# Steps 1 to 3 of the first product in a fused diffusion block: the next adaLN unit moved in front of the product with the activations' low half

## The chip, the cores and the metric

The kernel runs on one core of one Trainium2 chip. The metric is the device time of one execution in microseconds (us), the median of several runs. The engines named below are TensorE (PE in the profile; PEld is its loading of weights), VectorE (DVE), ScalarE (ACT), GpSimd (POOL) and the queue of SyncE (SP), which issues nearly all loads.

## The reference, cut to what matters

Two layers work on 256 latent tokens and 256 context tokens of width 1024. The change lies at the very start of the first layer: the adaLN map, the modulation of the tokens by it, and the first product of the Conformer module.

```python
def adaln(cvec, w, b):
    return jnp.split(jax.nn.silu(cvec) @ w + b, 6, axis=-1)

def modulate(x, shift, scale):
    return x * (1 + scale) + shift

def conformer_conv(u, rows, w_pw1, b_pw1, ...):
    a = u @ w_pw1 + b_pw1
    a = a[..., :CONV_DIM] * jax.nn.sigmoid(a[..., CONV_DIM:])
    ...
...
sh1, sc1, g1, sh2, sc2, g2 = adaln(c[:, None, :], ada_w[i], ada_b[i])
csh1, csc1, cg1, csh2, csc2, cg2 = adaln(c_ctx, ada_w[i], ada_b[i])
u = modulate(h, sh1, sc1)
uc = modulate(hc, csh1, csc1)
```

## The kernel before, in words

Context and latent tokens lie side by side as 512 columns, with the 1024 features in eight slabs of 128 partitions (`DT = 8`). Products are made in halves: each fp32 operand is split into a high part, rounded to the matmul's format, and a low part, the rest, and a product is three matmuls: high weight by high activation, high weight by low activation, low weight by high activation (`mm3`, lines 185, 188 and 189). `split` makes the halves of a weight (ScalarE casts the high one, line 154, VectorE subtracts to get the low one, line 155).

**The first product** is accumulated over the eight slabs in four blocks of 128 output columns, 0 to 3, each in a PSUM bank of its own (`ps0`); all four stay open over the eight steps. Step f needs the slab's scale and shift, and these come out of the adaLN weights step by step, in a chain:

- `start0(f)` (line 630) issues three loads on SP's queue (a 1 MB block of the adaLN weights into one of three buffers `raw`, the slab's part of the first weights, 256 KB, into one of five buffers `F`, the slab of x, 256 KB), then makes the adaLN *unit*: eight products on TensorE, 16 matmul records at line 342, into the PSUM bank `fl`. VectorE copies the bank out (line 646).
- `start1(f)` (line 648) splits the slab's weights, adds up the four partial sums of the unit with a matmul, the *fold* (line 350, into `ln`), turns them into shift and scale on VectorE (lines 655 and 656), and makes the modulated slab `u[f]` with `affine_split` (line 599): the high half on ScalarE and, for slabs 0 to 3, half of it on VectorE (lines 607 and 604), the same values in fp32 on VectorE (line 611), and last the low half, by a subtraction on VectorE (line 613).
- `start2(f, ms)` (line 672) makes the three matmuls of slab f for the blocks `ms`.

In step 0 the products of block 0, 1 and 2 are issued one by one by `part(ms, k)` (line 746): k = 0 is high by high, k = 1 low weight by high activation, k = 2 high weight by low activation. There part 2 comes behind the unit of slab 1.

In steps 1 to 3 the order on TensorE is: block 0 (three matmuls), the unit of slab f + 1, block 1, the fold of slab f + 1, blocks 2 and 3. The unit of slab 5 follows at the end of step 3; from step 4 on, the unit is two slabs ahead, and stands at the end of the step before. The order on TensorE and of the loads on SP's queue is pinned as written here (`keep_in_program_order`, and `pin[0]` for the units, folds and first matmuls of each `mm3`). The order on VectorE and ScalarE is not: the compiler of the kernel chooses it by priorities and a simulated time, held only by the edges that `issue_after` draws. So a chain of small additions (`foldg`, lines 787 and 789) with lowered priority has been put between step 1's low half and the next unit's copy, and a chain of sines (lines 682 to 695) among the splits that follow the first product.

After step 7 the other products of the Conformer module follow, and then the rest of the two layers; TensorE has work without a pause, and loads are issued when a buffer comes free.

Of the kernel before, what the change touches and what calls it, by code (L numbers as in the profile page):

```python
# [71 lines left out]
def hybrid_kernel(ctx: ExitStack, tc: tile.TileContext, xT, vecs_d, taps_d, bdw_d, ada0_w, ada_w, wg_d, pw1a, pw1, pw2, w1_0, w2_0,  # L72
                  w1_1, w2_1, up_x, up_z, wv, wo, bo_d, wk, wq, wqT, wdown, rows_d, out):
    nc = tc.nc
# [10 lines left out]
    def nm(s):  # L85
        uid[0] += 1
        return f"{s}_{uid[0]}"
# [13 lines left out]
    def psum(tag="mm"):  # L101
        return pp.tile([P, 512], F32, tag=tag, name=nm(tag), bufs={"mm": 3, "ln": 2, "fl": 1, "cv": 2}[tag])
# [81 lines left out]
    def mm3(ps, wh, wl, xh, xl, start, stop):  # L184
        a = nc.tensor.matmul(ps, wh, xh, start=start, stop=False)  # L185
        if pin[0]:
            tc.keep_in_program_order(a)
        nc.tensor.matmul(ps, wh, xl, start=False, stop=False)  # L188
        lastmm[0] = nc.tensor.matmul(ps, wl, xh, start=False, stop=stop).ins  # L189
# [30 lines left out]
    def kcol(w, kt):  # L220
        if isinstance(w[0], list):
            w, kt = (w[0][kt // 4], w[1][kt // 4]), kt % 4
        return w[0][:, kt * P:(kt + 1) * P], w[1][:, kt * P:(kt + 1) * P]
# [115 lines left out]
    def ada_mm(ps, blocks, v=0, first=True, last=True, kts=range(DT)):  # L339
        for kt in kts:  # L340
            j = kt % 4
            a = mark_unit[0] = nc.tensor.matmul(ps[32 * j:32 * j + 32], cs[:, kt, 14 - 2 * v:46 - 2 * v], blocks[kt],  # L342
                                 start=first and kt < 4, stop=last and kt >= 4, tile_position=(0, 32 * j))
            if pin[0]:
                tc.keep_in_program_order(a)
# [275 lines left out]
    x, u = [], []  # L621
    lastload = [None]
    KO0 = 4
    ps0 = [psum("cv" if m == 3 else "mm") for m in range(KO0)]
# [3 lines left out]
    st = {}  # L628

    def start0(f):  # L630
        t = X()
        raw = wp.tile([P, 2048], F32, tag="raw", name=nm("raw"), bufs=3)
        wr = F()
        loads = [(raw, ada0_w[f]), (wr[:, :KO0 * P], pw1a[f]), (t, xT[f * P:(f + 1) * P, :])]
        if f == 0:
            loads += [(bdw[:, 0:C], taps_d)]
        for d_, s_ in loads:
            lastload[0] = tc.keep_in_program_order(nc.sync.dma_start(d_, s_)).ins
        if f == 4:
            lastload[0] = tc.keep_in_program_order(nc.sync.dma_start(vecs[:, NV0:], vecs_d[:, NV0:])).ins  # L640
        x.append(t)
        ps = psum("fl")[:, :2 * P]
        ada_mm(ps, [raw[:, kt * 2 * P:(kt + 1) * 2 * P] for kt in range(DT)])
        sb = F()[:, :2 * P]
        with tc.issue_after(folded):
            st[f] = wr, sb, nc.vector.tensor_copy(sb, ps).ins

    def start1(f, then=lambda: None):
        if f:
            with tc.issue_after(st[f][2]), tc.issue_after(lastaff[0]):  # L650
                w = split_w(st[f][0][:, 0:KO0 * P])
        tr = ada_fold(st[f][1], 2 * P, tag="ln")
        then()
        with tc.issue_after(lastsub[0]) if f else nullcontext():
            nc.vector.tensor_scalar(sh1[:, :, f], tr[:, 0:2], vecs[:, o0 + f:o0 + f + 1], None, op0=ALU.add)
            sc_ = nc.vector.tensor_scalar(sc1[:, :, f], tr[:, 2:4], vecs[:, o0 + DT + f:o0 + DT + f + 1], 1.0,
                                          op0=ALU.add, op1=ALU.add)
        u.append((U(F32R), U(F32R)))
        if f:
            affine_split(*u[f], x[f], sc1, sh1, f, f < 4)  # L660
        else:
            def first_w():
                nonlocal w
                with tc.issue_after(lasthi[0]):
                    w = split_w(st[f][0][:, 0:KO0 * P])
                return lastsub[0]

            w = None
            affine_split(*u[f], x[f], sc1, sh1, f, True, first_w)
        st[f] = w  # L670

    def start2(f, ms):
        for m in ms:
            mm3(ps0[m], *kcol(st[f], m), *u[f], f == 0, f == DT - 1)
# [33 lines left out]
    keep = tc.keep_in_program_order  # L708
# [34 lines left out]
    start1(0, lambda: taps(banks))  # L743
    taps_out(banks)

    def part(ms, k):
        for m in ms:
            w_, x_ = kcol(st[0], m), u[0]
            keep(nc.tensor.matmul(ps0[m], w_[k == 1], x_[k == 2], start=k == 0, stop=False))

    part((0, 1), 0)
    part((0, 1), 1)
    part((2,), 0)
    part((2,), 1)
    start0(1)
# [2 lines left out]
    part((2,), 2)  # L758
    start2(0, (3,))
    for f in range(1, DT):  # L760
        start2(f, (0,))
        if f in (1, 2, 3):
            start0(f + 1)
            start2(f, (1,))
            start1(f + 1)
            start2(f, (2, 3))
        else:
            if f + 1 < DT:
                start1(f + 1)
            start2(f, (1, 2, 3))  # L770
        if 3 <= f and f + 2 < DT:
            start0(f + 2)
# [1380 lines left out]
```

## Time and profile before

| what | value |
|---|---|
| median of 3 runs | 1657.6 us (1657.56 to 1658.04) |
| the profiled execution | 1657.58 us, with a span of 1655.9 us |
| mean granted TensorE clock | 0.999 |
| ScalarE busy | 727.8 us (44%) |
| GpSimd busy | 14.3 us (1%) |
| read from HBM | 286.47 MB |

The span is the time from the first to the last record of the core; the rest of the execution's time lies around it. A timeline row gives the start and the length in us, the engine and line, the operation, output<-input with the tile names of the program, the shapes, and in brackets the idle time of the engine before it and what ended it. A row of waits gives who waited for whom, the total in us, how often, and the longest. A row of windows gives the stretch, its length, the busy time of each engine in it with its count, the granted clock, the share of the DMA engines and their GB/s. A matmul's length is modelled and overlaps the next one's, so the pace of matmuls is read from their starts.

### The profile page before, as it was taken

How to read it: one execution, taken by the hardware profiler on the slowest of the kernel's cores; microseconds unless marked ns; L12 is line 12 of the kernel's file. 1: busy time of each engine (PE TensorE's matmuls, PEld its weight loads, DVE VectorE, ACT ScalarE, POOL GpSimd, SP SyncE). 2: the span in 40 equal slices, each digit the busy share in tenths (PEclk: the TensorE clock that was granted, in tenths of full speed). 3: DMA queues.
4: the chain of work that ended last, by engine and by line, in shares of the span. 5: the costliest groups of instructions: out<-in, count | busy, mean ns of one | idle time of the engine just before them, and what ended most of it. 6: DMA issues, size and time to landing. Idle time of an engine off the chain costs nothing.

```text
span 1655.9 us, 22678 instructions
## 1 busy us (share of the span) xinstructions
PE 1642.1 (99%) x8818; PEld 1352.3 (82%) x8818; DVE 1045.7 (63%) x1884; ACT 727.8 (44%) x1170; POOL 14.3 (1%) x65
## 2 busy tenths in 40 slices
PE   8999999999999999999999999999999999999998
PEld 6665998888888998877787899888878888878887
DVE  6655895666535776762254753553489776776677
ACT  4313562232324475642233533442478654555453
POOL 0000000000000000000000000000000000000001
PEclk9999999999999999999999999999999999999999
DMA  8765313444324065557774852553466655685552
GB/s 342 252 228 220 115 64 122 150 139 147 118 102 153 9 233 190 190 194 278 283 247 151 293 179 86 178 192 143 151 226 220 212 212 205 237 288 182 178 188 92
DMA packets 80635, 305.81 MB, mean 185 GB/s; under 512 B 12012, under 2 KB 30352, under 8 KB 50576
## 3 DMA queue, kind: packets, MB, share of 16 engines
q1 hardware_dynamic: 58064, 288.07, 49.5%
q10 hardware_dynamic: 22464, 16.30, 3.1%
q8 instruction: 69, 1.13, 0.3%
q14 instruction: 38, 0.31, 0.1%
HBM read 286.47 MB, written 17.86 MB: 184 GB/s over the span
## 4 chain that ended last, share of the span: by engine, by line
PE 95%; DVE 2%; DMA 1%; ACT 1%; issue 0%; DVEq 0%; SPq 0%; ACTq 0%
PE mm L185 18%; PE mm L188 17%; PE mm L189 17%; PE mm L200 7%; PE mm L201 4%; PE mm L216 3%; PE mm L218 3%; PE mm L217 3%; PE fl L342 2%; PE cv L216 2%; PE cv L217 1%; PE cv L218 1%; PE ln L185 1%; PE cv L964 1%; PE ln L188 1%; PE fl L852 1%
## 5 line engine op out<-in xcount | busy, mean ns | idle before, releaser
L155 DVE TENSOR_TENSOR wl<-raw,wh 128x1024 fp32r<-128x1024 f32 x344 | 418.4, 1221 | 247.3 <-ACT wh L154 243.0
L154 ACT CAST wh<-raw 128x1024 fp32r<-128x1024 f32 x344 | 358.5, 1051 | 470.1 <-PE mm L188 247.3
L188 PE MATMUL mm<-u,wh 128*128 128x512 f32 (+1 forms) x805 | 290.6, 361 | 2.0 <-DVE u L613 2.0
L185 PE MATMUL mm<-u,wh 128*128 128x512 f32 (+1 forms) x677 | 242.1, 358 | 0.0
L189 PE MATMUL mm<-u,wl 128*128 128x512 f32 (+1 forms) x677 | 239.7, 354 | 0.0
L188 PEld LDWEIGHTS mm<-u,wh 128*128 128x128 f32 x805 | 152.0, 189 | 25.2 <-DVE u L613 3.5
L185 PEld LDWEIGHTS mm<-u,wh 128*128 128x128 f32 x677 | 127.8, 189 | 24.1 <-issue 4.7
L189 PEld LDWEIGHTS mm<-u,wl 128*128 128x128 f32 x677 | 127.9, 189 | 17.8
L216 PE MATMUL mm<-wh,xl 128*128 128x512 f32 x256 | 101.2, 395 | 0.8 <-ACT wh L154 0.8
L185 PE MATMUL mm<-xm,wh 128*128 128x512 f32 x256 | 101.0, 395 | 0.0
L217 PE MATMUL mm<-wh,xl 128*128 128x512 f32 x256 | 100.0, 391 | 0.0
L189 PE MATMUL mm<-xm,wl 128*128 128x512 f32 x256 | 99.7, 389 | 0.0
L218 PE MATMUL mm<-wl,xl 128*128 128x512 f32 x256 | 99.4, 392 | 0.2 <-DVE wl L155 0.2
L185 PE MATMUL mm<-hid,wh 128*128 128x512 f32 (+1 forms) x256 | 93.3, 364 | 0.0
L189 PE MATMUL mm<-hid,wl 128*128 128x512 f32 (+1 forms) x256 | 92.8, 363 | 0.0
L188 PE MATMUL mm<-hid,wh 128*128 128x512 f32 (+1 forms) x256 | 92.8, 363 | 0.0
L200 PE MATMUL mm<-x,wh 128*128 128x512 f32 x232 | 81.1, 398 | 0.0
L188 PE MATMUL mm<-qq,wh 128*128 128x272 f32 x256 | 73.9, 289 | 0.0
L185 PE MATMUL mm<-qq,wh 128*128 128x272 f32 x256 | 73.5, 288 | 0.0
L189 PE MATMUL mm<-qq,wl 128*128 128x272 f32 x256 | 73.5, 288 | 0.0
L200 PE MATMUL mm<-u,wh 128*128 128x512 f32 x192 | 68.6, 399 | 0.0
L1207 DVE SCALAR_TENSOR_TENSOR x<-mm,ada,x 128x256 f32<-128x256 f32 x64 | 28.5, 479 | 63.1 <-PE mm L189 63.1
(563 smaller groups left out, 3245.8 us busy)
## 6 DMA issues: line engine op xcount, KB each, us to landing
raw<-w SPq DMA_DIRECT2D x64, 1024.0 KB, 4.8
raw<-wo SPq DMA_DIRECT2D x32, 1024.0 KB, 4.9
raw<-ada_w SPq DMA_DIRECT2D x22, 1024.0 KB, 6.3
ar<-ada_w SPq DMA_DIRECT2D x80, 256.0 KB, 3.7
raw<-wv SPq DMA_DIRECT2D x16, 1024.0 KB, 7.5
raw<-wqT SPq DMA_DIRECT2D x16, 1024.0 KB, 6.2
raw<-wq SPq DMA_DIRECT2D x16, 1024.0 KB, 5.8
raw<-wk SPq DMA_DIRECT2D x16, 1024.0 KB, 4.9
```

Source lines behind the costliest of these rows:

```text
L154: c = nc.scalar.copy(hi, src)
L155: lastsub[0] = nc.vector.tensor_tensor(lo, src, hi.bitcast(F32), op=ALU.subtract).ins
L185: a = nc.tensor.matmul(ps, wh, xh, start=start, stop=False)
L188: nc.tensor.matmul(ps, wh, xl, start=False, stop=False)
L189: lastmm[0] = nc.tensor.matmul(ps, wl, xh, start=False, stop=stop).ins
L200: todo = [lambda s_, e_: nc.tensor.matmul(ps, wh, r[0], start=s_, stop=e_), lambda s_, e_: nc.tensor.matmul(ps[:, :n], wl, r[0][:, :n], st ...
L201: lambda s_, e_: nc.tensor.matmul(ps[:, :n], wl, r[0][:, :n], start=s_, stop=e_)]
L216: nc.tensor.matmul(ps, xh, wh, start=start, stop=False)
L217: nc.tensor.matmul(ps, xl, wh, start=False, stop=False)
L218: nc.tensor.matmul(ps, xh, wl, start=False, stop=stop)
L342: a = mark_unit[0] = nc.tensor.matmul(ps[32 * j:32 * j + 32], cs[:, kt, 14 - 2 * v:46 - 2 * v], blocks[kt], start=first and kt < 4, stop=l ...
L1207: nc.vector.scalar_tensor_tensor(res[m][:, sl_], p_, g[:, m:m + 1], res[m][:, sl_], op0=ALU.mult, op1=ALU.add)
```

## The change

In steps 1 to 3 block 0 is no longer done as a whole ahead of the unit of the next slab. Its products of the high activation half (high weight, then low weight) stay ahead of it; its product with the activations' low half comes behind it, ahead of block 1. For this `part` takes the slab as an argument. The three matmuls are the same; the low weight's product now comes second and not third. Steps 4 to 7 keep their order.

```diff
-    def part(ms, k):
+    def part(ms, k, f=0):
         for m in ms:
-            w_, x_ = kcol(st[0], m), u[0]
-            keep(nc.tensor.matmul(ps0[m], w_[k == 1], x_[k == 2], start=k == 0, stop=False))
+            w_, x_ = kcol(st[f], m), u[f]
+            keep(nc.tensor.matmul(ps0[m], w_[k == 1], x_[k == 2], start=k == 0 and f == 0, stop=False))
...
     for f in range(1, DT):
-        start2(f, (0,))
         if f in (1, 2, 3):
+            part((0,), 0, f)
+            part((0,), 1, f)
             start0(f + 1)
+            part((0,), 2, f)
             start2(f, (1,))
             start1(f + 1)
             start2(f, (2, 3))
         else:
+            start2(f, (0,))
             if f + 1 < DT:
                 start1(f + 1)
             start2(f, (1, 2, 3))
```

## Prediction

> **What bounds the kernel now.** I read the page's head first, then the list of what TensorE waited for over the whole span, then the first 45 us by timeline and by windows.
>
> ```profile
> span 1655.9 us, 22678 instructions
> PE 1642.1 (99%) x8818; PEld 1352.3 (82%) x8818; DVE 1045.7 (63%) x1884; ACT 727.8 (44%) x1170; POOL 14.3 (1%) x65
> ```
>
> TensorE is busy for 1642.1 of 1655.9 us. The list of its waits, whole span:
>
> ```profile
> PE mm L188 <- DVE u L613: 2.0, 3, 0.8
> PE fl L342 <- DMA raw<-ada_w: 1.2, 1, 1.2
> PE cv L179 <- DVE ones L138: 1.1, 1, 1.1
> PE mm L216 <- ACT wh L154: 0.8, 1, 0.8
> ```
>
> These are its four longest. The first is the change's target: three times, in steps 1, 2 and 3, the product with the low half (line 188) stood waiting for VectorE to finish that half (line 613). It is the largest wait that TensorE has, and still only 2.0 us. So the question is small: how much more than 2.0 us goes with it, and does any of it get lost before the end.
>
> The windows from each adaLN unit's start to the next one's (units 2 to 6):
>
> ```profile
> 16.85:22.15 5.30, 4.69 (x34) 2.96 (x33) 3.65 (x11) 1.11 (x2) 0.00 (x0) 1.00 1.01 393
> 22.15:27.46 5.31, 4.68 (x33) 2.96 (x32) 3.12 (x8) 1.11 (x2) 0.00 (x0) 1.00 1.05 412
> 27.46:31.17 3.71, 3.71 (x31) 2.48 (x30) 2.10 (x6) 0.98 (x2) 0.00 (x0) 1.00 1.02 407
> 31.17:35.57 4.40, 4.40 (x34) 3.04 (x33) 3.33 (x8) 2.23 (x5) 0.53 (x3) 1.00 1.03 409
> ```
>
> A step of the same work takes 5.30 and 5.31 us where the stall sits in it, and 4.40 us later, where none does (31.17:35.57). The granted clock is 1.00 in all four, so no clock goes into the sum. The DMA share is 1.0 throughout: the loads run at the limit of what this stage moves, about 400 GB/s, and that has to be watched.
>
> **The change, part by part.** The order of TensorE, step 1 in full and step 2's stall:
>
> ```profile
> 14.93 0.50 PE L185 MATMUL mm<-u,wh 128*128 128x512 f32 x1
> 16.19 0.50 PE L188 MATMUL mm<-u,wh 128*128 128x512 f32 x1 [0.75 <-DVE u L613]
> 16.53 0.40 PE L189 MATMUL mm<-u,wl 128*128 128x512 f32 x1
> 16.85 1.07 PE L342 MATMUL fl<-raw,cs 128*32 128x256 f32 x16
> 17.85 0.50 PE L185 MATMUL mm<-u,wh 128*128 128x512 f32 x1
> 18.19 0.40 PE L188 MATMUL mm<-u,wh 128*128 128x512 f32 x1
> 18.43 0.39 PE L189 MATMUL mm<-u,wl 128*128 128x512 f32 x1
> 18.65 0.50 PE L350 MATMUL ln<-fold,F 128*128 128x2 f32 x4
> 19.02 0.47 PE L185 MATMUL mm<-u,wh 128*128 128x512 f32 x1
> ...
> 20.48 0.40 PE L185 MATMUL mm<-u,wh 128*128 128x512 f32 x1
> 21.49 0.50 PE L188 MATMUL mm<-u,wh 128*128 128x512 f32 x1 [0.61 <-DVE u L613]
> 21.82 0.40 PE L189 MATMUL mm<-u,wl 128*128 128x512 f32 x1
> 22.15 1.07 PE L342 MATMUL fl<-raw,cs 128*32 128x256 f32 x16
> ```
>
> Nothing is removed and nothing added: the three matmuls of block 0 stay, and the unit's 16 records stay. What moves is the unit, from behind the stalled product to in front of it. The starts give the pace: a matmul after a wait or after a unit is followed 0.34 us later (16.19 to 16.53, 17.85 to 18.19), any other one 0.24 or 0.22 us later (18.19 to 18.43, 18.43 to 18.65), a low weight's product is followed by a unit after 0.32 us (16.53 to 16.85), a unit by a product after 1.00 us (16.85 to 17.85), and a fold by a product after 0.37 us (18.65 to 19.02).
>
> *Step 1.* High by high starts at 14.93 as before, since nothing ahead of it changes. Low weight by high activation follows at 15.27, the unit of slab 2 at 15.27 + 0.32 = 15.59, against 16.85: 1.26 us earlier. The product with the low half comes at 16.59.
>
> *Steps 2 and 3.* From unit to unit the new order is: unit 1.00; the low-half product 0.34; block 1, 0.24 + 0.24 + 0.22 = 0.70; fold 0.37; blocks 2 and 3, 1.46 (19.02 to 20.48); high by high 0.23 (the pace of blocks 1 to 3); low weight's product 0.32. Sum 4.42 us, beside the 4.40 of the undisturbed window. Units 3 and 4 then start at 20.01 and 24.43, against 22.15 and 27.46.
>
> *To unit 5.* Before, 3.71 us lie between units 4 and 5. After, the low-half product of block 0 lies there too: 3.71 + 0.24 = 3.95. Unit 5 starts at 28.38 and not at 31.17: **2.79 us** earlier. From there the order is the old one. The 2.79 is 2.0 of idle time, plus what the rows of idle time do not count: the wait begins at a matmul's modelled end, not at the pace of 0.23, and the matmul after each wait is a slow one.
>
> *Does the low half come in time?* The other engines of the chain, step 1 to 2:
>
> ```profile
> 15.44 0.69 DVE L613 TENSOR_TENSOR u<-S,u 128x512 fp32r<-128x512 f32 x1
> 16.05 0.17 DVE L787 TENSOR_TENSOR foldg<-ident 128x16 f32<-128x16 f32 x1
> 16.25 1.22 DVE L789 TENSOR_TENSOR foldg<-foldg,ident 128x16 f32<-128x16 f32 x6
> 17.99 0.42 DVE L646 COPY F<-fl 128x256 f32<-128x256 f32 x1 [0.52 <-PE fl L342]
> 18.33 0.68 DVE L155 TENSOR_TENSOR wl<-F,wh 128x512 fp32r<-128x512 f32 x1
> ...
> 19.58 0.60 ACT L607 ACTIVATE u<-x,sh1p,sc1p 128x256 fp32r<-128x256 f32 x1 [3.57 <-DVE sc1p L656]
> ...
> 20.74 0.69 DVE L613 TENSOR_TENSOR u<-S,u 128x512 fp32r<-128x512 f32 x1
> ```
>
> In step 1 the low half ends at 16.13, and the product now wants it at 16.59. In step 2 it ends 2.78 us after the fold's start (18.65 to 21.43). The new fold starts at 16.59 + 0.34 + 0.70 = 17.63, the low half ends at 20.41, and the product wants it at 20.01 + 1.00 = 21.01: 0.60 us of room. The high half ends 1.53 us after the fold's start (20.18), so at 19.16; high by high wants it at 15.59 + 1.00 + 0.34 + 0.70 + 0.37 + 1.46 = 19.46: 0.30 us of room, the smallest on this path. The low weights end 0.36 us after the fold's start (19.01), long ahead of their product, although it now comes second.
>
> *What the unit's new place makes wait.* The product with the low half, and behind it blocks 1 to 3 and the fold, now also stand behind the wait of the unit for its load. Before, only blocks 1 to 3 and the fold did.
>
> *What stood under the stall.* In step 1 VectorE filled its pause with seven `foldg` additions, 16.05 to 17.47, and the copy of the unit came behind them at 17.99. The copy trails the unit's start by 1.14 us, so it now wants to run at 16.73. If all seven additions stay ahead of it, it runs at about 17.40 to 17.82, and the fold at 17.88, not 17.63: 0.25 us lost, once. If they go behind, nothing or some tenths. I take 0.1, so **2.7 us** in all.
>
> *The loads.* Issue times, and us from that issue to landing, for the small weights of slab 2, then the blocks of units 4 and 5:
>
> ```profile
> 6.64 0.33 SPq L638 DMA_DIRECT2D F<-pw1a  x1
> ...
> 12.76 0.33 SPq L638 DMA_DIRECT2D raw<-ada_w  x1
> ...
> 17.98 0.33 SPq L638 DMA_DIRECT2D raw<-ada_w  x1
> ```
>
> ```profile
> F<-pw1a SPq DMA_DIRECT2D x1, 256.0 KB, 8.7
> ```
>
> ```profile
> raw<-ada_w SPq DMA_DIRECT2D x1, 1024.0 KB, 10.4
> ```
>
> ```profile
> raw<-ada_w SPq DMA_DIRECT2D x1, 1024.0 KB, 9.5
> ```
>
> Unit 2's block was queued ahead of the small weights, which land at 15.34, so it is there at 15.59. Unit 4's lands at 23.16 and is wanted at 24.43; unit 5's lands at 27.48 and is wanted at 28.38. That is the narrowest of the two, 0.90 us. The loads of units 5 to 7 are issued when a unit frees its buffer, so earlier; as the queue is full they land no earlier, but nothing makes them later either, if the queue is served in order. A step's loads are 1024 + 256 + 256 KB = 1.57 MB, 3.8 to 4.0 us at the 412 and 393 GB/s of the windows: below the new step of 4.42.
>
> *Does the gain reach the end?* Of TensorE's four longest waits only the one for `wh` at line 216 belongs to work after this stage, 0.8 us. Everything behind unit 5 is released by TensorE or by what follows it, and so moves with it. Against this speaks the Trainium skill, page Perfetto Trace Analysis, section Identifying the Most-Contended Engine: the matmul busy share is no good measure of how near TensorE is to its limit, the busy share of LDWEIGHTS is better. By that, 82% would leave room for the start's gain to be lost on the way, and the sum would be near 0. I go by the waits, which name almost nothing.
>
> The profiled execution took 1657.58 us, its span and 1.7 us around it, and the median of the runs is 1657.6, so the sum needs no correction: 1657.6 - 2.7 = **1654.9 us**. A change under 0.2%, 3.3 us here, is about what a measurement of this kernel can't tell from none.
>
> **The rivals.**
>
> *More than that: the later wait goes too.* What follows is compiled again, and the 0.8 us at line 216 may vanish by a new order: 2.8 + 0.8 = 3.6 us, 1654.0. For it: the order of VectorE and ScalarE is not written out. Against: nothing in the change aims at it.
>
> *The loads set the pace.* If the loads issued earlier share the bandwidth with unit 5's block, and do not queue behind it, that block may land later by up to one step's loads, 1.57 MB at 407 GB/s, 3.9 us: 31.3 against the 31.17 of before. The gain is gone: 1657.8. For it: the DMA share of 1.0. Against: that share held before as well, and the blocks landed about 10 us after their issue, as in a queue.
>
> *Given back later.* Some other wait takes it up by halves, or the pinned order is not what the compiler makes of it: 1656.2 to 1657.6.
>
> *Slower: the sines go ahead of a split.* After the first product VectorE runs three splits and then a chain of sines:
>
> ```profile
> 49.55 3.46 DVE L155 TENSOR_TENSOR wl<-raw,wh 128x1024 fp32r<-128x1024 f32 x3
> 52.92 0.36 DVE L682 TENSOR_SCALAR F<-tab 128x384 f32<-128x384 f32 x1
> ...
> 59.24 0.47 DVE L811 TENSOR_SCALAR tab<-tab,pc 128x256 f32<-128x256 f32 x1
> ```
>
> ```profile
> 53.14 0.39 PE L189 MATMUL mm<-u,wl 128*128 128x512 f32 x1
> ```
>
> The first of the three splits ends a third of 3.46 us after 49.55, at 50.7, and line 189 uses it at 53.14: 2.4 us of room. The sines take 52.92 to 59.71, 6.8 us. If TensorE runs earlier against loads that come no earlier, the compiler may put the sines ahead of that split: the product then waits 6.8 - 2.4 = 4.4 us, less 2.7 won, 1.7 us slower, 1659.3. It decides from 5.1 us of sines ahead of the split on. Against: all of it moves with TensorE.
>
> **How the numbers follow.** The forecast has 0.66; more than that 0.11; given back later 0.09; the loads 0.08; the sines 0.06. The range is 1653.8 to 1657.0: the forecast with both ends of the `foldg` term, the rival with more, and most of what is given back; the loads and the sines are left out above. Faster by over 0.2%: 0.15, the rival with more and an upper tail of 0.04. Slower: 0.04, since the sines at 1659.3 would still be within 0.2% and only a longer stall counts. Within: 0.81.
>
> **What would show it.** Right: no wait at line 188 for line 613 any more, units 2 to 5 starting near 15.6, 20.0, 24.4 and 28.4, steps of 4.4 us between them, and TensorE's last matmul 2.7 us earlier. Wrong: a wait of line 342 for a load of `ada_w`, a wait of line 350 for the copy, units in place but a new wait after 45 us, or steps longer than 4.5 us.

## The result and the profile after

The changed kernel takes 1654.84 us (median of 22 runs, 1654.0 to 1656.12), the kernel before 1657.72 us (22 runs beside them, 1656.96 to 1659.15). The ratio is 0.9983, with a 95% interval of 0.9976 to 0.999: 2.9 us, or 0.17%, faster. The whole interval lies below 1, so the kernel did get faster; whether by more than 0.2% it leaves open. The prediction was 1654.9 us.

The head of the page after, and the list of all of TensorE's waits:

```profile
span 1653.1 us, 22678 instructions
PE 1641.5 (99%) x8818; PEld 1352.4 (82%) x8818; DVE 1046.0 (63%) x1884; ACT 727.9 (44%) x1170; POOL 14.3 (1%) x65
```

```profile
PE cv L179 <- DVE ones L138: 1.1, 1, 1.1
PE fl L342 <- DVE E L692: 0.9, 1, 0.9
PE mm L216 <- ACT wh L154: 0.8, 1, 0.8
PE ln L217 <- DVE hid L155: 0.3, 1, 0.3
PE cv L967 <- DVE F L956: 0.3, 1, 0.3
PE ln L548 <- DVE ln L536: 0.2, 1, 0.2
```

The wait for the low half of the activations, 2.0 us before, is no longer in the list, neither at line 188 nor at line 749 (`part`), where that product now stands. The work of TensorE is the same, 1641.5 us against 1642.1. (Lines behind the change have moved down by three, so line 967 here is line 964 before.)

TensorE's timeline after, from the first product of step 1 to the unit of slab 3 and the product behind it:

```profile
14.61 0.50 PE L749 MATMUL mm<-u,wh 128*128 128x512 f32 x1
14.95 0.40 PE L749 MATMUL mm<-u,wl 128*128 128x512 f32 x1
15.27 1.07 PE L342 MATMUL fl<-raw,cs 128*32 128x256 f32 x16
16.27 0.50 PE L749 MATMUL mm<-u,wh 128*128 128x512 f32 x1
...
17.31 0.50 PE L350 MATMUL ln<-fold,F 128*128 128x2 f32 x4
17.67 0.47 PE L185 MATMUL mm<-u,wh 128*128 128x512 f32 x1
...
19.14 0.40 PE L749 MATMUL mm<-u,wh 128*128 128x512 f32 x1
...
19.69 1.07 PE L342 MATMUL fl<-raw,cs 128*32 128x256 f32 x16
20.69 0.50 PE L749 MATMUL mm<-u,wh 128*128 128x512 f32 x1
```

No row has a wait in brackets. Counted from the first product of step 1 (14.61 here, 14.93 before), unit 2 starts 0.66 us later, the fold 2.70, the next high by high 4.53; the prediction had 0.66, 2.70 and 4.53. The windows from unit to unit, 2 to 6:

```profile
15.27:19.69 4.42, 4.42 (x33) 3.04 (x32) 3.83 (x14) 1.63 (x3) 0.00 (x0) 1.00 1.02 405
19.69:24.11 4.42, 4.42 (x33) 3.04 (x32) 3.38 (x11) 0.78 (x2) 0.00 (x0) 1.00 1.03 403
24.11:28.07 3.96, 3.96 (x31) 2.66 (x30) 2.50 (x7) 1.45 (x3) 0.00 (x0) 1.00 1.02 407
28.07:32.49 4.42, 4.42 (x33) 3.04 (x32) 3.37 (x8) 2.21 (x5) 0.53 (x3) 1.00 1.02 411
```

Steps of 5.30 and 5.31 us have become 4.42 and 4.42, the 3.71 between units 4 and 5 has become 3.96, and in each window TensorE is busy for the whole of it. From the first product of step 1 to the start of unit 5 it takes 13.46 us (14.61 to 28.07), where it took 16.24 (14.93 to 31.17). This **stretch** is the yardstick below: it is **2.78 us** shorter, and unlike the total it does not hang on when the first unit started.

How the gain travels, by one product in the second half of the kernel and the last matmul of all, before and then after:

```profile
1209.62 0.39 PE L217 MATMUL mm<-wh,xl 128*128 128x512 f32 x1
...
1648.00 0.28 PE L218 MATMUL mm<-wl,hid 128*128 128x256 f32 x1
```

```profile
1206.53 0.39 PE L217 MATMUL mm<-wh,xl 128*128 128x512 f32 x1
...
1645.23 0.28 PE L218 MATMUL mm<-wl,hid 128*128 128x256 f32 x1
```

At unit 5 TensorE is 3.10 us ahead of before, at this product 3.09, at the end 2.77. So the lead is carried through some 1180 us unchanged. Two pieces of these numbers are not the change's. One is the 0.32 us at the first product of step 1: the first unit began at 6.42 and not at 6.76, and its load landed 5.0 us after its issue and not 5.4. The other is a wait of 0.3 us at line 217 near the end. In another trace of the changed kernel (the one timed below beside the unit first), the first product of step 1 starts at 14.99, almost as before, and the last matmul at 1645.14, 2.86 us earlier than before.

### The profile page after: what moved, and what is told of

Read it like the earlier page. It is cut to its first block, busy times and chain, and to the rows that moved or that the text cites. A ratio compares the mean times of both kernels' runs of the same rounds, so it can differ in the third digit from the quotient of the medians.

```text
span 1653.1 us, 22678 instructions
## 1 busy us (share of the span) xinstructions
PE 1641.5 (99%) x8818; PEld 1352.4 (82%) x8818; DVE 1046.0 (63%) x1884; ACT 727.9 (44%) x1170; POOL 14.3 (1%) x65
## 4 chain that ended last, share of the span: by engine, by line
PE 95%; DVE 3%; DMA 1%; ACT 1%; issue 0%; DVEq 0%; ACTq 0%
PE mm L185 18%; PE mm L188 17%; PE mm L189 17%; PE mm L200 7%; PE mm L216 4%; PE mm L218 4%; PE mm L217 4%; PE mm L201 3%; PE fl L342 2%; PE cv L216 2%; PE cv L218 1%; PE cv L217 1%; PE ln L185 1%; PE cv L967 1%; PE ln L188 1%; PE fl L855 1%
```

## The experiments

All counts are of the stretch from the first product of step 1 to the start of unit 5: 16.24 us before, 13.46 after. The theory: three separate stalls of TensorE on the low half are covered by the unit, each by its own step, and the rest of the kernel carries the sum. The rivals: a schedule that the compiler makes anew, the inner order of block 0 (and not the unit's place), and loads that set the pace. The pieces are about as small as what 11 runs can tell apart in the total, so they are read from the stretch of one trace each, and the total stands beside it.

### Step 1 alone

```diff
-        if f in (1, 2, 3):
+        if f in (1,):
             part((0,), 0, f) ... (the new order)
+        elif f in (2, 3):
+            start2(f, (0,)) ... (the old order)
```

> The new order in step 1 alone; steps 2 and 3 in the old order. Yardstick of all runs: the stretch from the first high by high product of step 1 to the start of unit 5, 16.24 us before (14.93 to 31.17) and 13.46 us after (14.61 to 28.07). Theory (the gain is made of three separate stalls, each removed by its own step's order, and the rest is carried unchanged): step 1 gives 1.02 us (fold at 17.63, not 18.65, on the clock of before), so the stretch is 15.22 and two waits of some 0.6 us for the low half stay, in steps 2 and 3. Rival (the gain comes from a schedule that the compiler makes anew once the order changes at all): the stretch or the total falls by much more or much less than a third of the whole, and the parts do not add up.

Measured: 14.57 to 29.83, 15.26 us, a gain of 0.98. Total 1656.95 us, ratio 0.9994 (0.9985 to 1.0003), which leaves no change open. The waits of TensorE on the low half, then the windows from unit to unit:

```profile
PE mm L188 <- DVE u L613: 1.2, 2, 0.6
```

```profile
15.24:20.79 5.55, 4.94 (x34) 3.15 (x34) 4.47 (x16) 1.64 (x3) 0.00 (x0) 1.00 1.02 409
20.79:26.11 5.32, 4.68 (x34) 2.96 (x33) 3.12 (x8) 1.12 (x2) 0.00 (x0) 1.00 1.01 397
```

Two waits are left of three, and step 3 still takes 5.32 us. Step 1's own stall is gone, and it gave what it should.

### Steps 2 and 3 alone

The same edit with `(2, 3)` in the new order and `(1,)` in the old.

> The new order in steps 2 and 3 alone; step 1 in the old order. Theory: one wait of 0.75 us stays, in step 1; units 3 and 4 come 4.18 and 4.42 us after the one before them; the stretch is 16.24 - 1.77 = 14.47 us, and with the run of step 1 alone the two gains add up to 2.79. Rival (a new schedule): they do not add up.

Measured: 14.58 to 29.07, 14.49 us, a gain of 1.75. Total 1656.09 us, ratio 0.999 (0.9981 to 0.9999). The one wait that is left, step 1's, then the windows:

```profile
PE mm L188 <- DVE u L613: 0.8, 1, 0.8
```

```profile
16.50:20.69 4.19, 4.19 (x32) 2.84 (x31) 3.25 (x11) 1.12 (x2) 0.00 (x0) 1.00 1.03 401
20.69:25.11 4.42, 4.42 (x33) 3.04 (x32) 3.12 (x9) 1.22 (x2) 0.00 (x0) 1.00 1.02 405
```

4.19 and 4.42, against 4.18 and 4.42 expected. The two parts give 0.98 + 1.75 = 2.73, the whole 2.78: they add up, as three separate stalls do. A schedule made anew would have no reason to.

### The inner order alone

```diff
             part((0,), 0, f)
             part((0,), 1, f)
-            start0(f + 1)
             part((0,), 2, f)
+            start0(f + 1)
```

> Block 0 in the new inner order in steps 1 to 3 (high by high, low weight by high activation, high weight by low activation), but whole and ahead of the unit. Theory (it is the unit ahead of the wait that matters, its 1.0 us of work; the low weight's product covers only its own 0.24 us): 0.24 us a step, the stretch is 16.24 - 0.72 = 15.52 us, the waits for the low half go from 2.0 to about 1.3 us in all. Rival (the low weight's product coming second is what does it): a stretch near 13.5.

Measured: 15.23 to 30.79, 15.56 us, a gain of 0.68. Total 1657.08 us, ratio 0.9995 (0.9986 to 1.0003), which again leaves no change open.

```profile
PE mm L749 <- DVE u L613: 1.3, 3, 0.5
```

```profile
16.91:21.99 5.08, 4.70 (x33) 3.04 (x32) 3.85 (x13) 1.11 (x2) 0.00 (x0) 1.00 1.01 395
```

All three waits stay, each shorter by the one matmul that now stands in front of it, and a step takes 5.08 us instead of 5.30. So the inner order alone gives a quarter of the gain, and the unit's place on top of it the other three quarters. The unit's place with the old inner order was not run. By the room worked out in the prediction, 0.46 us in step 1 and 0.60 in the others, of which the low weight's product makes up 0.23 to 0.34 by the pace of the rows, it would probably cover the stalls without the inner order too; that is an estimate.

### The unit ahead of all of block 0

```diff
+            start0(f + 1)
             part((0,), 0, f)
             part((0,), 1, f)
-            start0(f + 1)
             part((0,), 2, f)
```

> The unit of the next slab ahead of the whole of block 0 in steps 1 to 3. Theory (TensorE's own work is the bound once the unit covers the wait, and the loads leave 0.4 us): unit 2 starts 0.1 us before the first high by high product would, so there is no wait for the high half either; unit 5 starts at 28.03 on the clock of before, 3.14 us earlier, 0.35 better than the changed kernel, and the total is 1654.5. Rival (the loads set the pace once units come earlier; block 4 landed 0.97 us and block 5 0.57 us ahead of its unit in the changed kernel): waits of the units for their loads, steps of over 4.45 us, and no gain over the changed kernel or less.

This moves the unit in front of the stretch's first product, so it is counted from the last product of step 0: 14.48 to 28.09, 13.61 us, where the changed kernel takes 13.90 (14.17 to 28.07) and the one before 16.66 (14.51 to 31.17). That is 0.29 us better than the change.

```profile
14.80:19.22 4.42, 4.42 (x33) 3.04 (x33) 3.56 (x12) 1.29 (x3) 0.00 (x0) 1.00 1.05 415
19.22:23.65 4.43, 4.43 (x33) 3.04 (x32) 3.84 (x14) 1.22 (x2) 0.00 (x0) 1.00 1.01 397
```

TensorE is busy to the last hundredth of both windows, and no unit of these steps waits for its load: with this order, too, the loads do not set the pace. Total 1654.69 us, ratio 0.998 (0.9971 to 0.9989). It was run again beside the changed kernel on the same chip:

> The unit ahead of the whole of block 0, once more, beside the changed kernel on the same chip. Theory (the stretch to unit 5 is 0.29 us shorter than in the changed kernel and nothing behind it depends on the order): 0.3 us faster, too little to be told apart by these runs. Rival (what is won in the stretch is lost behind it): slower than the changed kernel.

> The changed kernel itself, timed beside the run with the unit first. Theory: 2.8 us under the kernel before, a ratio of 0.998, as in the result.

Measured: 1654.79 us, 0.9981 (0.9972 to 0.9989), for the unit first; 1655.23 us, 0.9984 (0.9975 to 0.9993), for the changed kernel. The stretch from the last product of step 0 is 13.61 us again against 13.89. The difference in the stretch is shown twice; in the total the intervals lie over each other.

### A later low half, in the old order and in the new

To measure the room, an instruction of the low half's chain is repeated on VectorE, in steps 1 to 3 only. It writes the same values again. Each of these runs is a single execution, so only the stretch is read from them.

```diff
-            for s, sl in HALVES:
+            for s, sl in HALVES + HALVES[1:] * (K if shared and f else 0):
                 nc.vector.tensor_scalar(t[:, sl], src[:, sl], ca[:, s, f:f + 1], cb[:, s, f:f + 1],
```

In the changed kernel, K = 1:

> The changed kernel, with one more of these VectorE instructions in each of steps 1 to 3: the low half comes 0.33 us later. Theory (the predicted room of the low half is 0.46 us in step 1 and 0.60 us in steps 2 and 3): nothing, the stretch stays at 13.46, no wait for the low half. Rival (the new order is as tight as the old one): 0.33 us a step, 14.4.

In the kernel before, K = 1:

> The kernel before with one more of the repeated VectorE instructions in each of steps 1 to 3, the counterpart of the changed kernel with one more. In that run a repeat took 0.45 us (three records of line 611 in 1.18 us, against two in 0.73). Theory (in the old order the low half has no room at all, and a stall this short leaves the granted clock at 1.00): 3 x 0.45 = 1.35 us, the stretch is 17.6 us, and the first wait is 1.2 us. Rival (some of the 2.0 us is not the low half's doing): less than 1.35. Rival (the old order is near the point where a stall lowers the clock, as three repeats did): more than 1.35, with a granted clock below 1.00.

Measured in the new order: 14.32 to 27.83, 13.51 us, 0.05 more than without. In the old order: 14.54 to 32.12, 17.58 us, 1.34 more. First the new order's windows, then the old one's wait and windows:

```profile
14.98:19.45 4.47, 4.47 (x33) 3.03 (x32) 3.93 (x15) 1.67 (x3) 0.00 (x0) 1.00 1.02 406
19.45:23.87 4.42, 4.42 (x33) 3.04 (x32) 3.88 (x13) 0.77 (x2) 0.00 (x0) 1.00 1.01 395
```

```profile
PE mm L188 <- DVE u L613: 3.3, 3, 1.2
```

```profile
16.91:22.66 5.75, 4.70 (x34) 2.96 (x33) 4.06 (x12) 1.12 (x2) 0.00 (x0) 1.00 1.01 390
22.66:28.40 5.74, 4.68 (x34) 2.96 (x33) 3.53 (x9) 1.12 (x2) 0.00 (x0) 1.00 1.04 415
```

The repeat took 0.45 us, not the 0.33 that was taken from the pace of two such instructions on different halves. In the old order each of the three shows in full: the low half has no room there. In the new order the first step loses 0.05 us (its room was put at 0.46, about what the repeat takes) and the others nothing. This is the plainest evidence of what the change does: the low half can now come later by 0.4 us in each step at almost no cost.

With K = 3, in the changed kernel:

> The changed kernel with three more of them: the low half comes 0.98 us later, past its room by some 0.5 us in step 1 and 0.4 in steps 2 and 3. Theory: waits for the low half are back, about 1.3 to 1.5 us in all, and the stretch is 14.9 us, against 2.9 us that the same three instructions cost in the old order. Rival (the room is larger than worked out, or the unit's copy on VectorE and the fold become the wait): no wait at the low half's product, or a wait at the fold.

Measured: 14.98 to 31.67, 16.69 us, where 14.9 was expected. The mechanism came as expected, waits at the low half's product, but more than twice the size. VectorE's rows in step 1 say why:

```profile
14.65 2.08 DVE L611 TENSOR_SCALAR S<-x,sc1p,sh1p 128x256 f32<-128x256 f32 x5
16.78 0.42 DVE L646 COPY F<-fl 128x256 f32<-128x256 f32 x1
17.12 0.68 DVE L613 TENSOR_TENSOR u<-S,u 128x512 fp32r<-128x512 f32 x1
```

Five instructions take 2.08 us, 1.35 more than two, and the compiler now put the next unit's copy (line 646) ahead of the low half, another 0.34 us (in steps 1 and 2, not in 3). So the price was mis-set, and VectorE's order, which nobody writes out here, did add to it.

With K = 3, in the kernel before:

> The kernel before, with three more VectorE instructions in each of steps 1 to 3, ahead of the low half (line 611's for the second half once more, thrice; they write the same values again). Line 611 takes 0.33 us from one to the next, so the low half comes 0.98 us later in each. Theory (in the old order TensorE waits for the low half in every step, and the next step starts that much later): all of it shows, 3 x 0.98 = 2.9 us, the stretch is 19.2 us. Rival (the chain has room elsewhere): less.

Measured: 14.62 to 38.87, 24.25 us, 8.0 more than without, where 2.9 was expected. The repeats were priced too low here as well: at the measured 1.35 us they would give 3 x 1.35 = 4.05 at full clock. The rest was not foreseen and is told of in the last section: the granted clock fell. From unit 2 to unit 3, at a mean clock of 0.53, it takes 8.59 us and not 5.30.

### The same program once more

> The changed kernel once more, for the two differences that the change does not explain: the first unit started 0.34 us earlier than in the kernel before, and near the end a wait of 0.29 us at line 217 for a low half of hid is there that was not. Theory (the first is how fast the first load came in that execution, the second the place of a VectorE instruction that the compiler moved): the first unit starts anywhere from 6.4 to 6.8 us, the second wait is there again. Rival (both belong to the single execution): both gone.

Measured: 1655.31 us, and a stretch of 13.46 us (14.52 to 27.98), the same to the hundredth. The first unit started at 6.33 us, and at 6.54 in the run beside the one with the unit first; the wait at line 217 was in neither. The wait at line 216, 0.8 us in the result, is longer here, and a new one stands at line 1759:

```profile
PE mm L216 <- ACT wh L154: 1.1, 1, 1.1
...
PE ln L1759 <- ACT og L1751: 0.4, 1, 0.4
```

So line 217's wait and the new one belong to the single execution, not to the program: the rival was right on line 217, and my theory that its wait came from a moved instruction has fallen. The start of the first unit belongs to the execution too: in the two runs of the old order with repeats it is 6.43 and 6.39, so the 6.76 of the trace before is not the old order's. What brings the late waits on was not looked into.

## Why the prediction was right

- *The sum.* 2.79 us to unit 5 was worked out. 2.78 came, in each of the three traces of the changed kernel against the one of before, out of 2.0 us of listed waits. Each step of it holds: steps of 4.42, unit 2 at 0.66 us behind the first product. The stretch between units 4 and 5 is 3.96 where 3.95 was said. The smallest room on the path, the high half's, was put at 0.30 us, and no product waits for that half. The reason that a wait of 2.0 us was worth 2.8 is shown by the same rows: the wait is listed from a matmul's modelled end, while the pace of matmuls is set by their starts, and the first matmul behind a wait is a slow one. By starts the three stalls before are 0.92, 0.78 and 0.79 us (16.19 - 14.93 less the usual 0.34 for the first), and each slow matmul behind them adds 0.1: 2.79.
- *The `foldg` term.* 0.1 us was taken off, and it cost nothing; without it the sum would have been 2.8. In VectorE's rows after, three additions stand ahead of the copy and the others in later pauses:

```profile
15.73 0.17 DVE L790 TENSOR_TENSOR foldg<-ident 128x16 f32<-128x16 f32 x1
15.93 0.39 DVE L792 TENSOR_TENSOR foldg<-foldg,ident 128x16 f32<-128x16 f32 x2
16.41 0.42 DVE L646 COPY F<-fl 128x256 f32<-128x256 f32 x1
```

  The copy starts 1.14 us behind the unit's start (15.27), as it did before (16.85 to 17.99).
- *The loads.* The queue's order held. Unit 5's block was issued 1.58 us earlier, at 16.40 and not at 17.98, and landed 11.1 us later and not 9.5:

```profile
16.40 0.33 SPq L638 DMA_DIRECT2D raw<-ada_w  x1
```

```profile
raw<-ada_w SPq DMA_DIRECT2D x1, 1024.0 KB, 11.1
```

  That is 27.5 us, the same as before, and its unit came 0.57 us behind; 0.90 was said, and most of the difference is the 0.32 us by which TensorE was already ahead. Of the rival that the loads set the pace nothing showed, here or with the unit first.
- *The way to the end.* TensorE passed on the gain unchanged, 3.10 us ahead at unit 5 and 3.09 at 1206 us. What was given back behind that is the 0.3 us at line 217, which the same program's other two traces do not have. So the 82% of weight loading, from which the Trainium skill's page Perfetto Trace Analysis (section Identifying the Most-Contended Engine) would judge TensorE's headroom, did not stand for slack that swallows a gain here; the list of waits was the better guide. The rival with more was not met either: line 216 still waits 0.8 us.
- *The sines* stayed behind the three splits, as they were. That rival was only not met; it was not tested.
- *The closeness.* That the time came out within 0.06 us is in part luck. The gain by the medians is 2.9 and not 2.7, and the kernel before measured 1657.72 over 22 runs where the forecast started from 1657.6; the two differences nearly cancel. Medians of one kernel also differ by more than that from one set of runs to the next (1654.84 and 1655.23 after; 1657.72, 1658.25 and 1658.01 before). The stretch is the better test.
- *What can be told apart.* The prediction took a change under 0.2% for one that a measurement can hardly tell from none. With 22 runs on each side 0.17% was told from none; 0.06% and 0.05%, with 11 runs of the changed program, were not.

## What to carry to other kernels

Where an engine that is otherwise never idle waits for the last of several inputs, split the work that waits by the inputs it needs, and put independent work that is due anyway in front of the last piece; the listed wait can then understate the gain (here 2.0 us were listed and 2.78 won). Measure the room of such a wait by a repeated instruction in the chain in front of it, one small enough not to change anything else: it showed in full in the old order and hardly at all in the new.

## What the runs showed of the hardware that was not expected

A short stall can cost more than itself. In the old order with three repeats, a single execution, TensorE waited 2.11 us in step 1, and the granted clock fell to half. Narrow windows put the fall between 16.1 and 16.3 us, about 1 us into the wait, and the return at 26.4. The timeline, then windows of 4 us:

```profile
14.62 0.49 PE L185 MATMUL mm<-u,wh 128*128 128x512 f32 x1
17.22 0.80 PE L188 MATMUL mm<-u,wh 128*128 128x512 f32 x1 [2.11 <-DVE u L613]
17.81 0.63 PE L189 MATMUL mm<-u,wl 128*128 128x512 f32 x1
18.37 1.94 PE L342 MATMUL fl<-raw,cs 128*32 128x256 f32 x16
20.24 0.80 PE L185 MATMUL mm<-u,wh 128*128 128x512 f32 x1
```

```profile
14.00:18.00 4.00, 1.85 (x6) 0.83 (x4) 3.65 (x12) 1.18 (x2) 0.00 (x0) 0.77 1.03 409
18.00:22.00 4.00, 4.00 (x24) 2.09 (x22) 1.45 (x5) 0.00 (x0) 0.00 (x0) 0.50 1.04 405
22.00:26.00 4.00, 3.73 (x10) 2.53 (x10) 3.18 (x9) 1.11 (x2) 0.00 (x0) 0.50 1.02 405
26.00:30.00 4.00, 3.78 (x29) 2.58 (x30) 1.85 (x6) 0.32 (x1) 0.00 (x0) 0.95 0.42 141
```

The unit takes 1.87 us from its start to the next product, not 1.00, and the clock is at 0.50 for two whole windows although TensorE works through the first of them. With waits of 1.20 and 1.05 us (one repeat), and of 1.15 (three repeats in the new order), it stayed at 1.00. The Trainium skill, page TensorE: Matmul & The Clock Gate, Part 1, has the clock fall after an idle window of about 3.4 us; here the clock fell at a wait of 2.11 us, with 1.85 us of work in the 4 us around it, and again just behind one of 1.95 us in step 3 of the same run (0.67 in the window from 34 to 38). Which lengths of wait are safe, and how it hangs on where the wait falls, these runs do not say: the first fall came after a shorter part of its wait than the 1.20 us that did no harm elsewhere. The stalls that the change removed were of 0.6 to 0.75 us, and the clock was no part of its gain.

Two instructions of VectorE that write the same place follow each other more slowly than two on different halves: a repeat took 0.45 us, where the second half follows the first after 0.33. A repeat also reads the same half again; which of the two makes it slower was not tested.
